# Block modulation beside w_out one chunk for one, and the first two feature tiles multiplied before their token factor

## The chip, the cores and the metric

The kernel runs on one core of one Trainium2 chip. The metric is device time in microseconds (us), the median over executions of the whole program. All tensors are fp32, and each weight matrix is read from HBM once.

## The reference, cut to what matters

One transformer layer acts on 128 context tokens and 256 latent tokens, 2048 features wide, so 384 tokens in three tiles of 128. The two groups differ in their conditioning vector (`c_ctx` or `c`), so everything that comes from the modulation exists twice, for the columns 0 to 127 and 128 to 383.

```python
mod = silu(c) @ w_mod + b_mod                  # w_mod: 2048 x 12288, six sections of 2048
shift1, scale1, gate1, shift2, scale2, gate2 = split(mod, 6)
h = rmsnorm(x, norm1) * (1 + scale1) + shift1   # rmsnorm: x * rsqrt(mean(x*x) + eps) * norm1
q, k, v, ... = split(h @ w_in)                  # w_in: 2048 x 10272
y = sigmoid(gate_a) * (y_a @ w_pa) + sigmoid(gate_b) * (y_b @ w_pb)
x = x + gate1 * (y @ w_out)                     # w_out: 2048 x 2048
h = rmsnorm(x, norm2) * (1 + scale2) + shift2
x = x + gate2 * ((silu(a) * b) @ w_down)        # a, b = halves of conv(h @ w_up)
```

The factor `rsqrt(mean(x*x) + eps)` belongs to a token and is called the factor of the tokens below. `norm1 * (1 + scale1)` and `shift1` belong to a feature.

## The kernel before, in words

**Chunks.** All weights pass through pieces of 512 KB, 128 partitions by 1024 numbers (`CK`), called chunks. A chunk is loaded on SyncE's queue (L340 to L345) into one of six buffers `raw`. Most chunks are then split in two parts: ScalarE rounds a half to fp32r (`hi`, L361), VectorE takes the rest (`lo`, L362), and TensorE makes three products of each pair of tiles, high by high, high by low and low by high (`mm3`, L370 to L373). There are five buffers for `hi` and five for `lo`. The list `chunks` is the order of the program; the loop `run` (L1246) walks it, loads up to five chunks ahead (`LD`), and splits two parts ahead (`SPL`). The compiler's scheduler then sets the order on each engine, and engines run their instructions in that order.

**The start.** SyncE's queue first takes the 18 pieces of the tokens (`xtok`, L97, 3.15 MB). The squares of all of them (`squares`, L103) give the factor of the tokens by a chain on VectorE (`rms_scale`, L189). The modulation for a feature tile of 128 (shift1 and scale1) takes four chunks of w_mod, multiplied on TensorE by `silu(c)` (`mb`, L227) and turned over through `finish` (L234). `prep_x` (L444) scales the tokens by their factor and transposes them (`sd`, L460, then `xn`), and `modulate` (L473) makes the input of the products, high part `xg` and low part `xl`.

**The first pass over w_in** makes q and k of both mixers, 24 tiles of 128 rows by 384 tokens, in nine stages by feature tiles (`STAGES`, L1116): one tile, one tile, then two at a time. Stage one and stage two have three chunks of w_in each, the later ones six. `SHARES` says after which chunk of w_in how many chunks of w_mod for the next stage stand. Each product is added from PSUM to the tile it belongs to (`evac_part`, L496): L502 and L500 copy in the first stage, L506 (VectorE, one instruction for 384 columns) and L504 add in the later ones. "Third stage" below means feature tiles 2 and 3.

**Block modulation on VectorE.** The other sections of w_mod (gate1, scale2, shift2, gate2) need no TensorE: `late_mod` (L252 to L265) multiplies each chunk by `silu(c)` on VectorE, four instructions of 128x512 for a chunk, adding into `lacc`. These are 128 chunks, 16 blocks of eight; they are called late chunks. After a block's eighth chunk `late_sum` (L287) sums over the partitions with 16 small products (L292). `spread` (L1095) puts late chunks among the main ones by a share for each phase (`dens`, L1201); `finish_late(b)` (L1195) puts all that are due and left, without main chunks between them.

**The second half.** The product by w_out goes by four column blocks of eight chunks; `spread` acts on the first five of each with share `dens[4]`. Results are gated and added to x (L924, L926), and the next block's first parts carry the second input's making (`scaled`, L944, with `hl`, L954). Then w_up goes in eleven groups of 16 chunks with share `dens[5]`, and from the third group on, after every second one, comes a group of w_down (16 chunks, products L428 to L430 with stationary `gh` and `gl`). Ahead of the first group of w_down stands `finish_late(4)` (L1228), because its gates need gate2.

Of the kernel before, what the change touches and what calls it, by code (L numbers as in the profile page):

```python
# [14 lines left out]
P = 128  # L15
# [20 lines left out]
def hybrid_step(  # L36
# [55 lines left out]
    xtok = []  # L92
    for t in range(3):
        row = []
        for (a, b) in XP:
            xt_ = slot("xtok")
            S.dma_start(out=xt_[:, :P * (b - a)], in_=xsrc[t][:, P * a:P * b])  # L97
            row.append(xt_)
        xtok.append(row)
# [3 lines left out]
    def squares():  # L103
        for t in range(3):
            for i, (a, b) in enumerate(XP):
                junk = sp.tile([P, NTOK], F32, name=nm("junk"), tag="pT", bufs=3)
                n = P * (b - a)
                if i % 3 == 2:
                    V.tensor_tensor(junk[:, :n], xtok[t][i][:, :n], xtok[t][i][:, :n], ALU.mult)
                    V.tensor_reduce(ssq1[:, t, i:i + 1], junk[:, :n], AX.X, ALU.add)  # L110
                else:
                    A.activation(junk[:, :n], xtok[t][i][:, :n], AF.Square, accum_out=ssq1[:, t, i:i + 1])
# [26 lines left out]
    squares()  # L139
# [66 lines left out]
    class Mod:  # L206
# [4 lines left out]
        def __init__(self, cols, width):  # L211
            self.cols, self.width, self.bank, self.n = cols, width, None, 0
            self.nk = CK // width
# [6 lines left out]
        def mm(self, raw, i, g):  # L220
            if self.bank is None:
                self.bank = s2p.tile([P, 2, 512], F32, name=nm("mb"), tag="sc")[:, 0]
            w = raw.rearrange("p (k c) -> p k c", k=self.nk)
# [111 lines left out]
    class Chunk:  # L335
        def __init__(self, src, shape, mm, split=True, by_rows=True):
            self.src, self.shape, self.mm, self.split, self.by_rows = src, shape, mm, split, by_rows
            self.raw, self.parts, self.need = None, [], None

        def load(self):  # L340
# [4 lines left out]
            S.dma_start(out=self.v, in_=self.src)  # L345

        def do_split(self, part):
# [12 lines left out]
            l = lo[:, :k * ncol].rearrange("p (k c) -> p k c", k=k)  # L360
            A.copy(h, v)  # L361
# [8 lines left out]
    def mm3(ps, wh, wl, xh, xl, first, last):  # L370
        T.matmul(ps, lhsT=wh, rhs=xh, start=first, stop=False)  # L371
        T.matmul(ps, lhsT=wh, rhs=xl, start=False, stop=False)  # L372
        T.matmul(ps, lhsT=wl, rhs=xh, start=False, stop=last)  # L373

# [21 lines left out]
    def partial_chunk(w, k0, nk, c0, evac):  # L396

        ncol = CK // nk

        def mm(ch, part):  # L400
            h, l = ch.parts[part]
            for i in range(ncol // P // PARTS):
                ps = mm_bank()[:, 0:NTOK]
                cs = slice(128 * i, 128 * i + 128)
                for kk in range(nk):
                    xh_, xl_ = xs1(k0 + kk)
# [34 lines left out]
    xl = [xp.tile([P, NX], R32, name=f"xl{k}", tag=f"xl{k}")[:, :NTOK] for k in range(KT)]  # L441
    xn = []

    def prep_x():  # L444
        tot = sp.tile([P, 3], F32, name="tot", tag="ssqa")
# [35 lines left out]
    def first_input(k0, nk):  # L481
        while len(xn) < k0 + nk:
            next(prep)
# [645 lines left out]
    for i, ch in enumerate(stage_mods(0)):  # L1129
        chunks.append(ch)  # L1130
        if i >= 2:
            mark(lambda: next(prep))
# [202 lines left out]
```

## Time and profile before

| what | value |
|---|---|
| median of 3 runs | 2313.24 us (2309.41 to 2313.98) |
| profiled execution, its own time | 2311.3 us |
| its span in the trace | 2309.6 us |
| TensorE busy | 2245.2 us, 97% of the span |
| VectorE busy | 1637.9 us, 71% |
| ScalarE busy | 1015.9 us, 44% |
| GpSimd busy | 146.5 us, 6% |
| chunks of w_mod, 512 KB each | 192, of them 128 late chunks |

The profiled execution lies 1.9 us under the median, inside the spread of the three runs. Times in the trace count from the start of the span; 1.7 us of the execution lie outside it. A product of 512 columns or 384 columns shows a "duration" longer than the step from one product to the next, since they are pipelined: the step is what counts in a dense stretch.

### The profile page before, as it was taken

Reading aid. Unit: us, or ns where it says so; the run is one execution under the profiler, and the core shown is the slowest. Engines: PE = TensorE matmul, PEld = TensorE weight load, DVE = VectorE, ACT = ScalarE, POOL = GpSimd, SP = SyncE. Lnnn points to the kernel's source line nnn. Section 1 sums busy time; section 2 is a strip of 40 time slices with the busy share of each in tenths; the row PEclk is TensorE's granted clock in tenths of the full one; section 3 lists DMA queues with packets and bytes.
Section 4 is the critical chain, followed back from the end, with each engine's and each line's share of the span. In section 5 each row is a group of like instructions: output and inputs, shape, how many; then the busy total and the mean of one; then the engine's idle time right before and its main releaser. Section 6 shows DMA issues by size and latency. Waiting matters only on the chain.

```text
span 2309.6 us, 34978 instructions
## 1 busy us (share of the span) xinstructions
PE 2245.2 (97%) x12814; PEld 2065.4 (89%) x12814; DVE 1637.9 (71%) x3413; ACT 1015.9 (44%) x2104; POOL 146.5 (6%) x261
## 2 busy tenths in 40 slices
PE   6999999999999999999999959999999999999998
PEld 5888997889999999987899958998899899989987
DVE  5777877777889989876789875565555555556576
ACT  5322355575555433333455522454344345434541
POOL 1000222211111100010000000000000000000000
PEclk9999999999999999999999979999999999999999
DMA  8787654445566677775656545444543543453462
GB/s 269 252 247 240 182 140 126 128 130 147 171 175 176 181 217 235 208 255 157 191 181 188 179 149 161 129 127 131 152 128 120 155 137 119 136 155 120 137 209 84
DMA packets 300300, 388.22 MB, mean 168 GB/s; under 512 B 17669, under 2 KB 215829, under 8 KB 300129
## 3 DMA queue, kind: packets, MB, share of 16 engines
q1 hardware_dynamic: 293552, 377.34, 53.6%
q0 software_dynamic: 5712, 7.09, 1.1%
q8 instruction: 100, 1.64, 0.3%
q10 hardware_dynamic: 864, 1.57, 0.2%
q14 instruction: 72, 0.58, 0.1%
HBM read 381.18 MB, written 4.76 MB: 167 GB/s over the span
## 4 chain that ended last, share of the span: by engine, by line
PE 89%; DVE 4%; DMA 3%; ACT 1%; issue 1%; POOL 0%; SPq 0%; DVEq 0%; ACTq 0%; POOLq 0%
PE mm L371 20%; PE mm L372 20%; PE mm L373 20%; PE mm L428 7%; PE mm L429 7%; PE mm L430 7%; DMA raw<-in_w_mod_dram 2%; DVE lacc L265 1%; PE mb L227 1%; DVE lo L362 1%; PE mm L1066 1%; PE mm L1065 1%; PE mm L1064 1%; PE sd L829 0%; DMA raw<-in_w_in_dram 0%
## 5 line engine op out<-in xcount | busy, mean ns | idle before, releaser
L361 ACT CAST hi<-raw 128x512 fp32r<-128x512 f32 x960 | 591.0, 620 | 1012.4 <-PE mm L372 526.4
L362 DVE TENSOR_TENSOR lo<-raw,hi 128x512 fp32r<-128x512 f32 x960 | 659.7, 693 | 482.3 <-ACT hi L361 478.3
L371 PE MATMUL mm<-hh,hi 128*128 128x386 f32 x1408 | 479.4, 340 | 0.0
L372 PE MATMUL mm<-hl,hi 128*128 128x386 f32 x1408 | 479.0, 340 | 0.0
L373 PE MATMUL mm<-hh,lo 128*128 128x386 f32 x1408 | 478.2, 340 | 0.0
L265 DVE SCALAR_TENSOR_TENSOR lacc<-raw,scT,lacc 128x512 f32<-128x512 f32 x480 | 342.0, 747 | 23.0 <-DMA raw<-in_w_mod_dram 22.8
L371 PE MATMUL mm<-xg,hi 128*128 128x384 f32 x1024 | 354.4, 347 | 2.2 <-ACT hi L361 1.4
L373 PE MATMUL mm<-xg,lo 128*128 128x384 f32 x1024 | 345.5, 337 | 0.0
L372 PE MATMUL mm<-xl,hi 128*128 128x384 f32 x1024 | 345.3, 337 | 0.0
L371 PEld LDWEIGHTS mm<-hh,hi 128*128 128x128 f32 x1408 | 267.7, 190 | 0.9 <-ACT hi L361 0.4
L372 PEld LDWEIGHTS mm<-hl,hi 128*128 128x128 f32 x1408 | 267.0, 190 | 0.2
L373 PEld LDWEIGHTS mm<-hh,lo 128*128 128x128 f32 x1408 | 266.6, 189 | 0.0
L371 PEld LDWEIGHTS mm<-xg,hi 128*128 128x128 f32 x1024 | 192.4, 188 | 21.9 <-issue 12.3
L428 PE MATMUL mm<-hi,gh 128*128 128x512 f32 x480 | 188.1, 398 | 15.3 <-ACT hi L361 14.8
L373 PEld LDWEIGHTS mm<-xg,lo 128*128 128x128 f32 x1024 | 192.2, 188 | 1.0 <-issue 0.8
L429 PE MATMUL mm<-lo,gh 128*128 128x512 f32 x480 | 190.5, 397 | 2.5 <-DVE lo L362 2.5
L372 PEld LDWEIGHTS mm<-xl,hi 128*128 128x128 f32 x1024 | 192.5, 188 | 0.5 <-issue 0.4
L430 PE MATMUL mm<-hi,gl 128*128 128x512 f32 x480 | 189.8, 395 | 0.0
L428 PEld LDWEIGHTS mm<-hi,gh 128*128 128x128 f32 x480 | 90.7, 189 | 37.1 <-ACT hi L361 15.0
L429 PEld LDWEIGHTS mm<-lo,gh 128*128 128x128 f32 x480 | 90.8, 189 | 23.8 <-DVE lo L362 3.0
L430 PEld LDWEIGHTS mm<-hi,gl 128*128 128x128 f32 x480 | 90.8, 189 | 21.5
L506 DVE TENSOR_TENSOR qk<-qk,mm 128x384 f32<-128x384 f32 x160 | 86.0, 549 | 25.0 <-PE mm L373 24.7
(333 smaller groups left out, 2974.0 us busy)
## 6 DMA issues: line engine op xcount, KB each, us to landing
raw<-in_w_mod_dram SPq DMA_DIRECT2D x192, 512.0 KB, 4.3
raw<-in_w_up_dram SPq DMA_DIRECT2D x176, 512.0 KB, 3.5
raw<-in_w_in_dram SPq DMA_DIRECT2D x160, 512.0 KB, 4.5
raw<-in_w_down_dram SPq DMA_DIRECT2D x80, 512.0 KB, 3.9
raw<-in_w_out_dram SPq DMA_DIRECT2D x32, 512.0 KB, 4.3
raw<-gate SPq DMA_DIRECT2D x28, 512.0 KB, 4.3
raw<-in_w_pb_dram SPq DMA_DIRECT2D x16, 512.0 KB, 3.8
raw<-in_w_pa_dram SPq DMA_DIRECT2D x16, 512.0 KB, 4.4
```

The costliest lines, as they stand in the source:

```text
L227: T.matmul(self.bank[32 * q:32 * q + 32, 0:self.width], lhsT=scT[:, k, 2 - 2 * i:34 - 2 * i], rhs=w[:, kk], start=i == 0 and k < 4, stop=i ...
L265: V.scalar_tensor_tensor(acc[:, j], w[:, kk], col, acc[:, j], ALU.mult, ALU.add)
L361: A.copy(h, v)
L362: V.tensor_tensor(l, v, h.bitcast(F32), ALU.subtract)
L371: T.matmul(ps, lhsT=wh, rhs=xh, start=first, stop=False)
L372: T.matmul(ps, lhsT=wh, rhs=xl, start=False, stop=False)
L373: T.matmul(ps, lhsT=wl, rhs=xh, start=False, stop=last)
L428: T.matmul(ps, lhsT=xh_[:, ts_], rhs=h[:, kk], start=k == ks[0], stop=False)
L429: T.matmul(ps, lhsT=xh_[:, ts_], rhs=l[:, kk], start=False, stop=False)
L430: T.matmul(ps, lhsT=xl_[:, ts_], rhs=h[:, kk], start=False, stop=k == ks[-1])
L506: V.tensor_tensor(dst[h][:, :NTOK], dst[h][:, :NTOK], ps, ALU.add)
L1064: T.matmul(ps, lhsT=gh[:, ts_], rhs=h, start=k == KL[0], stop=False)
```

## The change

**Late chunks.** `dens[4]` goes from .5 to 1. In the program's list of loads, before, 86 late chunks stand ahead of the first chunk of w_out, 10 between there and the first chunk of w_up, and 32 between there and the first of w_down: 24 of these stand among the chunks of w_up, and the last eight, a whole block, behind them. Now the same three numbers are 86, 20 and 22, and all 22 stand among the chunks of w_up.

**Tokens.** Only the first of six column pieces of the tokens (feature tiles 0 to 2) is loaded ahead of the weights; the other five are loaded behind chosen chunks (`then`, `load_x`). The squares of a piece are taken by ScalarE alone, behind an instruction that waits for a result of the first stages (`behind`).

**Products without the factor.** The first two feature tiles (`NRAW`) are transposed unscaled (`raw_tile`), multiplied by `norm1 * (1 + scale1)`, and get two more columns with `shift1` (`raw_input`, 386 columns in all); they are kept in the tiles of `xl` that are used last. Their products are summed over two stages, then GpSimd multiplies the 24 sums by the factor of the tokens (`times_r`), spread over the partitions by `token_row`. The third stage adds its products and the shift columns, with two VectorE instructions where one was (L573 in the changed kernel), and for the four tiles of `qa` with two more on ScalarE. The modulated inputs of tiles 0 and 1, which later phases need, are made in the third stage (`first_input(0, 2)`).

**Splits.** Among the first 20 chunks, a part is split only when its chunk is the next one, and chunks that are not split let a split happen too (`split_ahead`).

On SyncE, at the start of the program, the queue holds these loads (`xtok` are pieces of the tokens, `raw` are chunk buffers). Before:

```order
L97 DMA xtok_120<-in_x_sample_dram 128x384
L97 DMA xtok_122<-in_x_sample_dram 128x384
L97 DMA xtok_124<-in_x_sample_dram 128x128
L345 DMA raw_226<-in_w_mod_dram 128x8x128
L345 DMA raw_228<-in_w_mod_dram 128x8x128
L345 DMA raw_230<-in_w_mod_dram 128x8x128
L345 DMA raw_232<-in_w_mod_dram 128x8x128
L345 DMA raw_234<-in_w_in_dram 128x1024
```

These three loads of tokens are the last of 18. In the changed kernel the queue begins, behind the constants, with:

```order
L98 DMA xtok_90<-in_x_prompt_dram 128x384
L98 DMA xtok_92<-in_x_sample_dram 128x384
L98 DMA xtok_94<-in_x_sample_dram 128x384
L346 DMA raw_154<-in_w_mod_dram 128x8x128
L346 DMA raw_156<-in_w_mod_dram 128x8x128
L346 DMA raw_158<-in_w_mod_dram 128x8x128
L346 DMA raw_160<-in_w_mod_dram 128x8x128
L346 DMA raw_162<-in_w_in_dram 128x1024
L346 DMA raw_164<-in_w_in_dram 128x1024
L98 DMA xtok_166<-in_x_prompt_dram 128x384
```

Three loads of tokens stand ahead of the first weights instead of 18, and the next ones follow behind the second chunk of w_in.

On VectorE, at the end of w_up's third group (`z` are the convolution's results, `lacc` the sums of a block of late chunks, `lo_14833` the low part of the first chunk of w_down), before:

```order
L991 SCALAR_TENSOR_TENSOR z_14712<-u_14711,cw,z_14712 128x255
L265 SCALAR_TENSOR_TENSOR lacc_14731<-raw_14599,scT,lacc_14731 128x512 x2
L265 SCALAR_TENSOR_TENSOR lacc_14731<-raw_14633,scT,lacc_14731 128x512 x4
L265 SCALAR_TENSOR_TENSOR lacc_14731<-raw_14639,scT,lacc_14731 128x512 x4
L265 SCALAR_TENSOR_TENSOR lacc_14731<-raw_14673,scT,lacc_14731 128x512 x4
L265 SCALAR_TENSOR_TENSOR lacc_14731<-raw_14723,scT,lacc_14731 128x512 x4
L265 SCALAR_TENSOR_TENSOR lacc_14731<-raw_14729,scT,lacc_14731 128x512 x4
L265 SCALAR_TENSOR_TENSOR lacc_14731<-raw_14736,scT,lacc_14731 128x512 x4
L265 SCALAR_TENSOR_TENSOR lacc_14731<-raw_14742,scT,lacc_14731 128x512 x4
```

and six rows further on `lo_14833`. In the changed kernel (`lo_14853` is the first part of w_down there):

```order
L1061 SCALAR_TENSOR_TENSOR z_14702<-u_14701,cw,z_14702 128x255
L368 TENSOR_TENSOR lo_14790<-raw_14639,hi_14789 128x512
L1060 SCALAR_TENSOR_TENSOR z_14718<-u_14717,cw,z_14718 128x127
L1060 SCALAR_TENSOR_TENSOR z_14718<-u_14717,cw,z_14718 128x255
L1061 SCALAR_TENSOR_TENSOR z_14718<-u_14717,cw,z_14718 128x127
L1061 SCALAR_TENSOR_TENSOR z_14718<-u_14717,cw,z_14718 128x255
L368 TENSOR_TENSOR lo_14819<-raw_14673,hi_14818 128x512
L368 TENSOR_TENSOR lo_14835<-raw_14673,hi_14834 128x512
L282 TENSOR_TENSOR lev_14802<-lev_14802,brow_14856 128x128 x2
L368 TENSOR_TENSOR lo_14853<-raw_14727,hi_14852 128x512
```

The eight late chunks between w_up and w_down are gone from this place, and the first part of w_down is split right behind the last parts of w_up.

On VectorE, in the third stage of the first pass (`qk` are the 24 tiles of q and k, `mm` the products in PSUM, `xl` the low part of the third stage's input), before:

```order
L362 TENSOR_TENSOR lo_822<-raw_729,hi_821 128x512
L506 TENSOR_TENSOR qk_339<-qk_339,mm_825 128x384
L506 TENSOR_TENSOR qk_345<-qk_345,mm_833 128x384
L362 TENSOR_TENSOR lo_842<-raw_729,hi_841 128x512
L506 TENSOR_TENSOR qk_351<-qk_351,mm_845 128x384
L506 TENSOR_TENSOR qk_357<-qk_357,mm_853 128x384
```

and in the changed kernel:

```order
L368 TENSOR_TENSOR lo_839<-raw_746,hi_838 128x512
L573 SCALAR_TENSOR_TENSOR qk_260<-qk_260,mm_842 128x128
L573 SCALAR_TENSOR_TENSOR qk_260<-qk_260,mm_842 128x256
L573 SCALAR_TENSOR_TENSOR qk_266<-qk_266,mm_851 128x128
L573 SCALAR_TENSOR_TENSOR qk_266<-qk_266,mm_851 128x256
L368 TENSOR_TENSOR lo_861<-raw_746,hi_860 128x512
L573 SCALAR_TENSOR_TENSOR qk_272<-qk_272,mm_864 128x128
L573 SCALAR_TENSOR_TENSOR qk_272<-qk_272,mm_864 128x256
```

Between two splits stand four instructions instead of two.

The diff, cut to its core:

```diff
+    def load_x(i):
+        a, b = XP[i]
+        for t in range(3):
+            xtok[t][i] = slot("xtok")
+            S.dma_start(out=xtok[t][i][:, :P * (b - a)], in_=xsrc[t][:, P * a:P * b])
+    load_x(0)
-    def squares():
+    def squares(i, behind=None):
+        if behind:
+            A.copy(ssq1[:, :, i], behind()[:, 0:3])
...
     def partial_chunk(w, k0, nk, c0, evac):
+        xs, n = (xs0, NX) if k0 < NRAW else (xs1, NTOK)
...
+    def times_r(x):
+        if "r" in first:
+            G.tensor_tensor(x[:, :NTOK], x[:, :NTOK], first["r"], ALU.mult)
+        else:
+            first.setdefault("wait", []).append(x)
+    def raw_input(k):
+        if k not in x0:
+            raw_tile(k)
+        scale_of(0, 1, k, k + 1)
+        x, (h, l) = x0[k], (xlx[KT - 2 - 2 * k], xlx[KT - 1 - 2 * k])
+        x0[k] = (h, l)
+        for j, (a, b) in enumerate(SEGS):
+            A.activation(h[:, a:b], x[:, a:b], AF.Copy, scale=sc_[:, 0, k, j:j + 1])
+            V.scalar_tensor_tensor(l[:, a:b], x[:, a:b], sc_[:, 0, k, j:j + 1], h[:, a:b].bitcast(F32),
+                                   ALU.mult, ALU.subtract)
...
+        elif k0 < NRAW:
...
+            times_r(dst[h])
+        elif k0 == NRAW and dst is not qa:
+            for j, (a, b) in enumerate(SEGS):
+                V.scalar_tensor_tensor(dst[h][:, a:b], dst[h][:, a:b], dst[h][:, NTOK + j:NTOK + j + 1], ps[:, a:b],
+                                       ALU.add, ALU.add)
...
-    SHARES = ((0, 2, 2), (0, 3, 5)) + ((0, 2, 2, 2, 2, 0),) * 7
+    SHARES = ((0, 0, 4), (0, 3, 5)) + ((0, 2, 2, 2, 2, 0),) * 7
...
+            if (st, i) == (2, 3):
+                mark(lambda: first_input(0, 2))
...
+            for g in squared.get((st, i), ()):
+                mark(lambda g=g: squares(*g))
+            if (st, i) == (1, 0):
+                mark(first_scale)
...
+    for i, at in enumerate((5, 7, 9, 10, 11)):
+        early[at].then = lambda i=i: load_x(i + 1)
+    early[10].behind = early[11].behind = lambda: kb[7]
...
-    dens = (.25, .25, .75, .8, .5, .5)
+    dens = (.25, .25, .75, .8, 1, .5)
```

More of the change, by code (lines that the diff above doesn't have):

```diff
@@ L337, in __init__ @@
             self.src, self.shape, self.mm, self.split, self.by_rows = src, shape, mm, split, by_rows
-            self.raw, self.parts, self.need = None, [], None
+            self.raw, self.parts, self.need, self.then, self.behind = None, [], None, None, None
         def load(self):
@@ L440, in hybrid_step, with token_row @@
     xh = [xg[k // 4][:, k % 4] for k in range(KT)]
-    xl = [xp.tile([P, NX], R32, name=f"xl{k}", tag=f"xl{k}")[:, :NTOK] for k in range(KT)]
-    xn = []
-    def prep_x():
+    xlx = [xp.tile([P, NX], R32, name=f"xl{k}", tag=f"xl{k}") for k in range(KT)]
+    xl = [x[:, :NTOK] for x in xlx]
+    xn = {}
+    x0 = {}
+    first = {}
+    def token_row(rs):
+        ps = sd_bank()
+        for t in range(3):
+            dg = sp.tile([P, P], F32, name=nm("dg"), tag="sqj")
+            V.tensor_scalar(dg, ident, rs[:, t:t + 1], None, ALU.mult)
+            T.matmul(ps[:, 128 * t:128 * t + 128], lhsT=ones, rhs=dg, start=True, stop=True)
+        return ps[:, :NTOK]
@@ L451, in prep_x, with xs0 @@
+    def xs0(k):
+        return x0[k]
+    def prep_x():
+        rs, scaled_ = first["rs"], set()
+        for k in (2, 3, 0, 1) + tuple(range(4, KT)):
+            if k // 3 not in scaled_:
+                scaled_.add(k // 3)
                 n = P * (XP[k // 3][1] - XP[k // 3][0])
@@ L481, in first_input @@
     def first_input(k0, nk):
-        while len(xn) < k0 + nk:
+        while any(k not in xn for k in range(k0, k0 + nk)):
             next(prep)
-        scale_of(0, 1, k0, k0 + nk)
+        if k0 >= NRAW:
+            scale_of(0, 1, k0, k0 + nk)
         for k in range(k0, k0 + nk):
@@ L972, in second_scale @@
         V.memset(r[:, NTOK:NX], 1.0)
-        ps = sd_bank()
-        for t in range(3):
-            dg = sp.tile([P, P], F32, name=nm("dg"), tag="sqj")
-            V.tensor_scalar(dg, ident, rs[:, t:t + 1], None, ALU.mult)
-            T.matmul(ps[:, 128 * t:128 * t + 128], lhsT=ones, rhs=dg, start=True, stop=True)
-        A.copy(r[:, :NTOK], ps[:, :NTOK])
+        A.copy(r[:, :NTOK], token_row(rs))
     za, gs = {}, {}
@@ L1255, in loads, with split_ahead @@
                 done["load"] += 1
+        place = {id(c_): i for i, c_ in enumerate(real)}
+        FIRST = 20
+        def split_ahead(pos, n):
+            while done["split"] < min(n, len(splits)):
+                ch, p_ = splits[done["split"]]
+                if ch.raw is None or pos + 1 < place[id(ch)] < FIRST:
+                    break
+                ch.do_split(p_)
+                done["split"] += 1
         pos = at = 0
@@ L1266, in run @@
                 for part in range(PARTS):
-                    while done["split"] < min(at + 1 + SPL, len(splits)):
-                        ch, p_ = splits[done["split"]]
-                        if ch.raw is None:
-                            break
-                        ch.do_split(p_)
-                        done["split"] += 1
+                    split_ahead(pos, at + 1 + SPL)
                     due()
```

85 lines of the change are left out of this document (52 added, 33 removed).

## The prediction

> **What bounds the kernel now.** I read the first page of the profile first: shares of the engines and the 40 slices.
>
> ```profile
> PE 2245.2 (97%) x12814; PEld 2065.4 (89%) x12814; DVE 1637.9 (71%) x3413; ACT 1015.9 (44%) x2104; POOL 146.5 (6%) x261
> PE   6999999999999999999999959999999999999998
> PEclk9999999999999999999999979999999999999999
> ```
>
> TensorE (PE) is the bound. Only two of the 40 slices (57.7 us each) fall under 8: the first, with 6, and the 24th, with 5, where the granted clock falls too. The change touches both. So I looked next at the busy time by windows around 1350 us, with one window from the second change from w_up to w_down, at 1586 us, for comparison.
>
> ```profile
> core 0: us, PE busy (x) PEld busy (x) DVE busy (x) ACT busy (x) POOL busy (x), PEclk, DMA share, GB/s
> 1350.00:1360.00 10.00, 3.89 (x35) 3.37 (x33) 7.13 (x16) 3.18 (x7) 0.00 (x0) 0.91 0.02 2
> 1360.00:1370.00 10.00, 1.35 (x3) 0.83 (x3) 10.00 (x16) 1.14 (x2) 0.00 (x0) 0.50 0.69 206
> 1370.00:1380.00 10.00, 1.97 (x17) 0.82 (x16) 9.77 (x19) 3.05 (x6) 0.70 (x2) 0.50 0.66 192
> 1580.00:1590.00 10.00, 10.00 (x53) 9.27 (x52) 6.12 (x13) 5.19 (x11) 0.00 (x0) 1.00 0.38 107
> ```
>
> PE stands nearly idle from 1354 to 1380 us while VectorE (DVE) is full, and the memory moves 2 GB/s in the first of these windows. At 1586 us the same change of phase costs PE nothing. The timeline of four engines says why (PE, then DVE, ACT, and SyncE's queue):
>
> ```profile
> 1353.22 0.66 PE L292 MATMUL sd<-lacc,ones 128*32 128x128 f32 x16
> 1368.65 1.65 PE L428 MATMUL mm<-hi,gh 128*128 128x512 f32 x3 [14.76 <-ACT hi L361]
> 1376.90 1.67 PE L292 MATMUL sd<-lacc,ones 128*32 128x128 f32 x16 [6.60 <-DVE lacc L265]
> 1381.08 0.80 PE L429 MATMUL mm<-lo,gh 128*128 128x512 f32 x1 [2.50 <-DVE lo L362]
> ...
> 1385.51 0.42 PE L429 MATMUL mm<-lo,gh 128*128 128x512 f32 x1
> ...
> 1386.00 0.39 PE L428 MATMUL mm<-hi,gh 128*128 128x512 f32 x1
> 1386.23 0.40 PE L429 MATMUL mm<-lo,gh 128*128 128x512 f32 x1
> ```
> ```profile
> 1357.46 19.96 DVE L265 SCALAR_TENSOR_TENSOR lacc<-raw,scT,lacc 128x512 f32<-128x512 f32 x30
> ```
> ```profile
> 1367.98 1.14 ACT L361 CAST hi<-raw 128x512 fp32r<-128x512 f32 x2 [11.88 <-DMA raw<-in_w_down_dram]
> ```
> ```profile
> 1364.20 5.67 SPq L345 DMA_DIRECT2D raw<-in_w_down_dram  x3
> ```
>
> The block of eight late chunks holds all six chunk buffers. DVE needs 30 instructions, 19.96 us, to empty them; the first chunk of w_down can be asked for only at 1364.20, ACT splits it at 1367.98, and its low parts stand behind the late chunks in DVE's order. PE then starts at a granted clock of 0.50.
>
> **The burst is taken away.** In the changed order no late chunk stands there, and the first parts of w_down are split behind the last of w_up, as at 1586 us. What it costs now: from 1381.08 to 1385.51 stand ten products of w_down in the trace, and three stood at 1368.65, so 13 are issued by 1385.5. At the step of 0.23 us (1386.00 to 1386.23) 13 take 3.0 us. The sums L292 are done at 1353.9, and the second set of them, 0.66 us warm, stays. So the 13th would be out at 1353.9 + 0.7 + 3.0 = 1357.6: **28 us less**. Its cover is DVE's slack in w_up; if that were missing it would come back as a part of the 20 us.
>
> **Ten late chunks move into w_out.** The late chunks there go from 10 to 20. The groups of DVE over that phase, and the phase as one window:
>
> ```profile
> 988.00:1122.00 134.00, 132.92 (x622) 108.51 (x621) 95.91 (x175) 47.78 (x93) 5.54 (x12) 1.00 0.63 202
> ```
> ```profile
> L362 DVE TENSOR_TENSOR lo<-raw,hi 128x512 fp32r<-128x512 f32 x63 | 42.9, 688 | 30.5 <-ACT hi L361 30.3
> L265 DVE SCALAR_TENSOR_TENSOR lacc<-raw,scT,lacc 128x512 f32<-128x512 f32 x48 | 34.0, 745 | 5.8 <-DMA raw<-in_w_mod_dram 5.8
> L954 DVE SCALAR_TENSOR_TENSOR hl<-sd,sc__224,hh 128x128 fp32r<-128x128 f32 (+1 forms) x24 | 8.9, 411 | 0.4
> ```
>
> One late chunk costs DVE 4 x 0.67 = 2.7 us in a row (19.96 us for 30), so ten add 27 us to 96 of 134 us: 123, or 92%. On average that fits. But the late chunks stand in the first five chunks of each of four blocks, where PE takes 134/32 = 4.2 us a chunk and DVE 2 x 0.69 for the splits and 2.7 for the late one, 4.1 us. On top come, from the block before, eight instructions L954 (24 over three blocks; 3.3 us) and six that gate, 512 columns each, priced as splits (4.1 us). These 7.4 us meet a lead of two split parts, one chunk of PE, 4.2 us; 3.2 us are over, unless late chunks wait instead of splits, and the last three chunks, which have no late one, make up 8 us. DVE also waits in order for late chunks to land (5.8 us now); ten more would be about as much again. Bounds: nothing, if late chunks take all the waiting, to 3.2 us in each of three blocks, 10 us. I take **3 us more**, nearer the low end, because of the 30.5 us in which DVE waits for ACT: there ACT waits for PE to free `hi`, so DVE has its full lead. Traffic rises from 202 GB/s by 5.2 MB over 134 us to 241, under what the start reaches (324, below).
>
> **The start.** These windows and timeline rows (ACT, then PE) are the start of the program:
>
> ```profile
> 20.00:30.00 10.00, 8.98 (x74) 6.32 (x74) 3.55 (x10) 7.15 (x18) 0.00 (x0) 1.00 1.15 324
> 30.00:40.00 10.00, 10.00 (x96) 8.93 (x95) 4.29 (x11) 9.58 (x23) 0.00 (x0) 1.00 0.78 265
> 40.00:50.00 10.00, 10.00 (x76) 9.01 (x75) 7.96 (x17) 4.46 (x11) 0.00 (x0) 1.00 0.66 217
> 50.00:60.00 10.00, 8.63 (x77) 6.71 (x76) 6.96 (x16) 1.41 (x3) 0.00 (x0) 1.00 0.92 304
> ```
> ```profile
> 9.47 0.28 ACT L135 ACTIVATE scT<-sd 128x16 f32<-128x16 f32 x2
> ```
> ```profile
> 21.66 1.08 PE L227 MATMUL mb<-raw,scT 128*32 128x128 f32 x16 [0.64 <-DMA raw<-in_w_mod_dram]
> ...
> 26.64 1.15 PE L371 MATMUL mm<-xg,hi 128*128 128x384 f32 x4
> ...
> 62.90 0.62 PE L227 MATMUL mb<-raw,scT 128*32 128x256 f32 x2 [0.68 <-DMA raw<-in_w_mod_dram]
> 63.45 0.44 PE L371 MATMUL mm<-xg,hi 128*128 128x384 f32 x1
> ```
>
> The fourth chunk of w_mod is multiplied at 21.66 us behind 18 loads of tokens. Without 15 of them (2.55 MB of 3.15) it is there 2.55 MB / 0.3 MB per us = 8.5 us sooner, at 13.2; `silu(c)` is ready at 9.75, and three chunks at 1.08 us fit between. The first product moves from 26.64 to about 18 us. But the tokens must still come before the third stage, whose first product, at 63.45, stands right behind a chunk of w_mod waited for at 62.90: there the memory ends last. The bytes up to that point are the same in both kernels, so 8.5 us are not kept. What is kept is the time in which the queue now runs below its rate, because buffers wait for a late PE: from 30 to 50 us it moves 265 and 217 GB/s between neighbours of 324 and 304. The shortfall is (314 - 265 + 314 - 217) x 10 us = 1.46 MB, at 314 GB/s **4.6 us less** to the third stage. Bounds: 2 us, if half of the dip stays, to 7, if the first ten microseconds fill too.
>
> **The third stage pays back.** Its window, and DVE's group there that is split in two:
>
> ```profile
> 63.50:95.80 32.30, 32.30 (x222) 29.04 (x222) 27.17 (x56) 10.35 (x19) 0.00 (x0) 1.00 0.78 249
> ```
> ```profile
> L506 DVE TENSOR_TENSOR qk<-qk,mm 128x384 f32<-128x384 f32 x23 | 12.3, 549 | 3.0 <-PE mm L373 2.9
> ```
>
> DVE has 27.2 of 32.3 us. Twenty tiles change from one L506 (0.55 us) to a pair; the pair L954 (128 and 256 columns, mean 0.41) takes 0.82, so 20 x 0.27 = 5.4 us. The inputs of tiles 0 and 1 add six instructions of up to 384 columns, priced as L506: 3.3 us. And GpSimd (POOL) multiplies 24 tiles meanwhile. What POOL does to DVE shows where POOL rotates q and k, at 260 us: the low parts L362 of the whole run, then those of 260 to 270 us (min, median, max), and POOL's own price.
>
> ```profile
> L362 DVE TENSOR_TENSOR lo<-raw,hi x960: 654/691/1225, 24.9 to 2254.1; 128x512 fp32r<-128x512 f32 x192
> ```
> ```profile
> L362 DVE TENSOR_TENSOR lo<-raw,hi x4: 761/922/1078, 261.0 to 269.4; 128x512 fp32r<-128x512 f32 x4
> ```
> ```profile
> L523 POOL TENSOR_TENSOR qk<-qk,cst 128x256 f32<-128x256 f32 x16 | 13.5, 846 | 0.0
> ```
>
> A split takes 0.23 us more beside POOL, 0.53 at most; the 12 splits of the stage give 2.8 us, at most 6.4. DVE: 27.2 + 5.4 + 3.3 + 2.8 = 38.7 us, over the 32.3 that PE takes. Of the 6.4 over, the four PSUM banks of `mm` and the slack of the fourth stage take some. I take **4 us more**, bounds 1 and 9. POOL itself: 24 x 0.846 x 1.5 = 30 us, from about 51 us (the factor needs the last tokens and a place on PE before stage two ends) to 81; the third stage asks for the tiles in the same order until 90, so POOL is covered by some 8 us. What is late next is DVE's adding, which frees PE's banks.
>
> The Trainium skill's page "SBUF — State Buffer", section "Who interferes with whom", speaks against this step: VectorE with two SBUF inputs and GpSimd reading SBUF exclude each other, and the second waits for the whole instruction. The 1.08 us split above agrees in kind. Taken in full it is the first rival below.
>
> **Sum.** 28 + 4.6 less, 3 + 4 more: 25.6 us. Against the profiled execution of 2311.3 us that is 2285.7; the median before, 2313.24, is 1.9 higher, so 2287.6, rounded down to **2287 us**. No difference under 0.2% (4.6 us) could be told from none.
>
> **Rivals.**
> - *POOL holds DVE for whole products.* If each of the 24 products (1.27 us) cost DVE half its length, 15 us come in place of 2.8; the third stage takes 12 us longer. For it: splits of up to 1.225 us. Against: the median beside POOL is 0.92. Time: about 2299 us. Chance 0.10.
> - *w_out becomes DVE's.* Late chunks that land late and wait for `lacc`'s one buffer stop DVE in order, with the splits behind: the 10 us of the bound, 2294 us. For it: 5.8 us of waits for landing. Chance 0.15.
> - *The third stage absorbs it.* DVE's lag disappears in the slack; the start keeps 6 us and w_out costs nothing: 2280 us. Chance 0.13.
> - *Slower than before: the block's work is not hidden anywhere.* If each of the ten moved late chunks put its whole 2.7 us on PE's path, since DVE has no slack left in the first five chunks of a block, the 28 us come back as 27; with the third stage at its bound of 9 more and the start at its bound of 2 less the time is 2313.2 - 28 + 27 + 9 - 2 = 2319. It decides when DVE's demand there passes PE's 4.2 us a chunk by more than the last three chunks make up, 8 us a block. Against: 92% on average. Chance 0.03.
> - *The stall at 1354 stays*, since the last late chunks of w_up still hold buffers: 2308 us or so. Against: the order. Chance 0.02.
>
> **Numbers.** The forecast has 0.57. Its own range is 2281 to 2293. The range for 8 in 10 takes in the absorbing rival and most of w_out's: 2278 to 2297. Faster by over 0.2%: 0.96; within: 0.01; slower: 0.03.
>
> **What would show it.** Right: in the changed profile PE runs at 10.00 of 10 us through the first change from w_up to w_down, with no L265 (now L266) run of 20 us and the clock at 1.00; the first product near 18 us; the third stage starts near 59 us and lasts about 36, with DVE full. Wrong: PE gaps over 1 us at the blocks of w_out behind DVE's low parts or `lacc`; the third stage longer than 41 us; or a start of the third stage later than 62 us.

## The result, and the profile after

| | before | after |
|---|---|---|
| median | 2312.9 us (4 runs, 2309.4 to 2314.0) | 2297.4 us (4 runs, 2295.5 to 2300.0) |
| ratio | 1 | 0.9936, 95% interval 0.9919 to 0.9953 |
| profiled execution, its span | 2311.3, 2309.6 us | 2296.4, 2294.7 us |

The change is faster by some 15 us and not by 25.6. The forecast of 2287 us is missed, and its range ends 0.4 us below the median. Of the kernels further below, tokens_only, no_factor, warm and shift_dve had one execution each of 3127 to 5644 us in a slow state, which is left out of their medians. The page of after, its totals and two rows of the 40 slices:

```profile
PE 2246.3 (98%) x12826; PEld 2066.9 (90%) x12826; DVE 1643.8 (72%) x3430; ACT 1024.4 (45%) x2141; POOL 173.3 (8%) x285
PE   7899999999999999999999999999999999999998
PEclk9999999999999999999999999999999999999999
```

The 5 in the 24th slice is gone, the first slice is 7 where it was 6. The windows around the first w_down, in which PE stood nearly idle before:

```profile
1350.00:1360.00 10.00, 10.00 (x70) 9.55 (x69) 7.39 (x17) 6.65 (x14) 0.00 (x0) 1.00 0.36 107
1360.00:1370.00 10.00, 10.00 (x58) 9.96 (x57) 3.41 (x6) 3.08 (x6) 1.99 (x4) 1.00 0.39 109
1370.00:1380.00 10.00, 10.00 (x45) 8.09 (x44) 8.18 (x18) 5.95 (x12) 0.00 (x0) 1.00 0.46 138
```

PE is full and the clock is 1.00. So the loss is elsewhere. To find it I laid the phases of all traces beside each other, by the first product of each phase. Times count from the start of the span. The third stage begins with the 145th product of the first pass, since stages one and two have 72 each. `add_xstat` is the function that makes the products of the pass over w_in behind the first one. "w_out's stretch" runs from the first product of w_out to the first of w_up, and the last column from there to the first product of the next group of w_up:

| trace | first product | third stage | fourth stage | add_xstat | w_out's stretch | first w_up and w_down |
|---|---|---|---|---|---|---|
| before | 26.6 | 65.6 | 95.8 | 275.2 | 142.1 | 305.2 |
| after | 18.5 | 71.6 | 104.3 | 285.6 | 148.2 | 275.8 |
| late_only | 26.7 | 64.9 | 95.7 | 275.8 | 148.4 | 276.2 |
| tokens_only | 19.8 | 73.0 | 105.7 | 286.3 | 142.6 | 304.5 |
| late_in_up | 25.7 | 64.0 | 94.1 | 274.3 | 141.4 | 277.0 |
| no_factor | 18.9 | 64.6 | 95.8 | 276.4 | 148.3 | 275.3 |
| pool_beside | 17.9 | 69.8 | 101.2 | 282.7 | 146.8 | 275.8 |
| factor_dve | 19.5 | 76.3 | 110.2 | 288.9 | 144.7 | 275.6 |
| warm | 20.1 | 64.5 | 95.7 | 277.2 | 146.0 | 275.2 |
| squares_dve | 19.3 | 63.4 | 94.6 | 274.5 | 146.6 | 275.2 |
| no_behind | 19.8 | 67.3 | 97.7 | 278.3 | 151.2 | 275.2 |
| shift_dve | 18.6 | 71.9 | 106.6 | 286.1 | 145.3 | 275.6 |
| tokens_best | 18.5 | 76.6 | 108.5 | 289.8 | 143.9 | 276.6 |
| late_half | 26.9 | 64.9 | 95.1 | 274.6 | 144.8 | 276.2 |
| late_quarter | 26.6 | 64.5 | 94.7 | 274.5 | 143.6 | 276.1 |
| late_double | 26.6 | 65.5 | 95.7 | 274.9 | 147.7 | 305.4 |

Between before and after: 29.4 us less around the first w_down, 6.1 more in w_out, **10.4 more up to add_xstat**, and 2.1 less in later work whose order did not change (not followed up). With 0.2 more between add_xstat and w_out that is 14.8 us less, which is what the spans differ by. The start, forecast at 0.6 us less, became the largest loss. Each row is one execution, and PE's first instruction stands 7.4 to 9.3 us after the start of the span in these traces, so a difference of 1 or 2 us between two rows says little. (The expectations below count from that instruction, set to 7.53 us. Their 70.9, 63.5 and 284.9 us are 71.6, 64.6 and 285.6 in this table.)

PE's rows in after show both ends of that loss (in brackets, how long PE stood idle and for what):

```profile
18.53 1.01 PE L377 MATMUL mm<-xl,hi 128*128 128x386 f32 x2 [2.76 <-ACT xl L497]
...
71.60 0.41 PE L377 MATMUL mm<-xg,hi 128*128 128x384 f32 x1 [2.27 <-DVE qk L568]
```

The first product comes 8.1 us sooner, the third stage 6 us later. All that PE waited for from 55 to 72 us in after (us in total, times, longest), then the same from 55 to 65 us in no_factor, the changed kernel without GpSimd's products (below):

```profile
PE mm L377 <- DVE qk L566: 3.3, 3, 2.2
PE mm L377 <- DVE qk L568: 2.3, 1, 2.3
PE mm L379 <- DVE lo L368: 0.9, 1, 0.9
```
```profile
PE mb L228 <- DMA raw<-in_w_mod_dram: 0.2, 1, 0.2
```

In after that is 6.5 us, all of it for VectorE. The windows between the two ends (columns as in the prediction: PE, PEld, DVE, ACT, POOL, clock, DMA, GB/s):

```profile
20.00:30.00 10.00, 9.31 (x39) 8.98 (x39) 0.00 (x0) 7.00 (x19) 0.00 (x0) 0.75 1.11 347
30.00:40.00 10.00, 7.76 (x98) 6.92 (x97) 4.05 (x11) 9.33 (x32) 0.00 (x0) 1.00 0.66 218
40.00:50.00 10.00, 10.00 (x73) 8.99 (x72) 8.57 (x23) 6.35 (x25) 0.00 (x0) 1.00 0.80 271
50.00:60.00 10.00, 8.54 (x72) 5.40 (x70) 8.89 (x23) 6.88 (x15) 4.19 (x4) 1.00 1.04 350
60.00:70.00 10.00, 5.94 (x45) 3.40 (x44) 10.00 (x16) 3.06 (x6) 10.00 (x10) 1.00 0.59 178
70.00:80.00 10.00, 8.40 (x39) 8.43 (x40) 8.12 (x16) 3.79 (x10) 10.00 (x10) 0.83 0.48 159
```

Three things stand out. The memory still runs at 218 and 271 GB/s from 30 to 50 us, so the dip stayed. From 60 to 70 us PE has 5.94 of 10 us while DVE and POOL are both at 10.00. DVE has only 16 instructions there. In the last row the clock is 0.83: behind PE's pauses it ran at half speed again, from 72.9 us on, which takes 1.7 us of PE's work from these 10 us, inside the third stage. DVE's groups from 45 to 71 us, with the mean of one in ns behind the comma, and POOL's:

```profile
L368 DVE TENSOR_TENSOR lo<-raw,hi 128x512 fp32r<-128x512 f32 x6 | 6.4, 1093 | 0.0
L568 DVE TENSOR_TENSOR qk<-qk,mm 128x386 f32<-128x386 f32 x11 | 6.0, 551 | 0.0
L536 DVE TENSOR_SCALAR hf<-xn,sc__152,mod 128x128 f32<-128x128 f32 (+1 forms) x4 | 3.6, 968 | 0.0
...
L539 DVE TENSOR_TENSOR xl<-hf,xg 128x384 fp32r<-128x384 f32 x2 | 2.2, 1114 | 0.0
```
```profile
L477 POOL TENSOR_TENSOR qk<-qk,r 128x384 f32<-128x384 f32 x24 | 27.1, 1165 | 46.7 <-ACT r L471 46.7
```

A split that takes 0.69 us elsewhere takes 1.09 on average (1.51 at most). The input of the third stage (`hf`, then `xl`) takes 2.6 and 2 times as long as it does without POOL (rows of no_factor, below).

### The profile page after: what moved, and what is told of

The parts are those of the page before. It is cut to its first block, busy times and chain, and to the rows that moved or that the text cites. A ratio compares the mean times of both kernels' runs of the same rounds, so it can differ in the third digit from the quotient of the medians.

```text
span 2294.7 us, 35120 instructions
## 1 busy us (share of the span) xinstructions
PE 2246.3 (98%) x12826; PEld 2066.9 (90%) x12826; DVE 1643.8 (72%) x3430; ACT 1024.4 (45%) x2141; POOL 173.3 (8%) x285
## 4 chain that ended last, share of the span: by engine, by line
PE 88%; DVE 5%; DMA 3%; issue 1%; ACT 1%; POOL 0%; DVEq 0%; ACTq 0%; POOLq 0%
PE mm L377 20%; PE mm L378 20%; PE mm L379 20%; PE mm L438 7%; PE mm L439 7%; PE mm L440 7%; DMA raw<-in_w_mod_dram 2%; DVE lacc L266 1%; DVE lo L368 1%; PE mb L228 1%; DMA raw<-in_w_out_dram 1%; PE mm L1136 1%; DMA raw<-in_w_in_dram 1%; PE mm L1135 1%; PE mm L1134 1%
## 5 line engine op out<-in xcount | busy, mean ns | idle before, releaser
L378 PE MATMUL mm<-xl,hi 128*128 128x384 f32 (+1 forms) x1024 | 347.4, 339 | 0.1
L377 PE MATMUL mm<-xg,hi 128*128 128x384 f32 x976 | 338.4, 347 | 3.4 <-DVE qk L568 2.3
L379 PE MATMUL mm<-xg,lo 128*128 128x384 f32 x976 | 330.0, 338 | 0.0
L377 PEld LDWEIGHTS mm<-xg,hi 128*128 128x128 f32 x976 | 183.7, 188 | 21.5 <-issue 15.2
L379 PEld LDWEIGHTS mm<-xg,lo 128*128 128x128 f32 x976 | 183.7, 188 | 1.1 <-issue 0.8
L438 PE MATMUL mm<-hi,xg 128*128 128x256 f32 (+1 forms) x288 | 96.7, 336 | 0.0
```

The lines of the kernel that those rows point to most:

```text
L438: T.matmul(ps, lhsT=xh_[:, ts_], rhs=h[:, kk], start=k == ks[0], stop=False)
```

## The experiments

Each ratio stands against the kernel before on the same chip (medians 2311.1 to 2311.5 us there, 2312.9 beside after). So where a run is compared with after, the difference is taken from the ratios, in parts of 2311 us.

**The two halves apart: late_only and tokens_only.** late_only is the kernel before with one edit, tokens_only is the changed kernel with the opposite one:

```
-    dens = (.25, .25, .75, .8, .5, .5)
+    dens = (.25, .25, .75, .8, 1, .5)
```

> The kernel before with w_out's share of late chunks set to one to one, and nothing else. If the two halves of the change simply add, this one leaves out the start's loss of 9.7 us that the two traces show (add_xstat's first product 275.2 to 284.9 us) and keeps the 6.0 us lost in w_out and the 29.4 us won around the first w_down: 2313 - 29.4 + 6.0 = about 2289 us. Rival: the 6.0 us of w_out come from the token half (what the first stages leave behind), so they go too: 2284 us. Second rival: the start's loss is made up later in any case, and this kernel is no better than the changed one: 2297 us.

> The changed kernel with w_out's share of late chunks put back to one to two: the start alone. If the halves add: 2313 + 9.7 = about 2322 us, with PE's stall before the first w_down back. Rival (the w_out loss belongs to this half): 2328 us. Second rival (made up later): 2313 us.

Measured: late_only 2287.5 us (ratio 0.990, 0.9887 to 0.9913), tokens_only 2320.7 us (1.0042, 1.0027 to 1.0057). The halves add: 23.7 less and 9.5 more make 14.2 less, where the whole change gave some 15. The second half of the change alone is slower than doing nothing, and the w_out loss stays with the late chunks (148.4 against 142.6 us).

**The late chunks in w_up: late_in_up.** The kernel before, with `dens = (.25, .25, .75, .8, .5, .69)`.

> The kernel before with w_out's share left at one to two and the share of the three first groups of w_up raised from .5 to .69, so that the 8 chunks of the burst go among w_up's products and none is added to w_out. Theory (a late chunk costs only where VectorE has no slack, and w_up's first groups have it: VectorE busy 174 of 206 us there, and 8 chunks of four operations of 0.744 us add 24): the 29 us come in full and no 6 us are lost, 2284 us. Rival (VectorE at 198 of 206 us makes TensorE wait as in w_out, 0.6 us a chunk or more): 2289 to 2294 us, with gaps on TensorE between 1144 and 1350 us.

Measured: 2281.8 us (0.987, 0.9857 to 0.9884), the fastest of all kernels here that compute everything. PE's windows at the change to w_down, and w_up's first three groups as one window:

```profile
1345.00:1355.00 10.00, 10.00 (x68) 9.20 (x66) 7.62 (x15) 4.75 (x10) 0.00 (x0) 1.00 0.73 250
1355.00:1365.00 10.00, 10.00 (x45) 8.11 (x44) 7.31 (x17) 4.54 (x8) 1.99 (x4) 1.00 0.32 108
```
```profile
1143.00:1351.80 208.80, 208.80 (x1216) 206.88 (x1215) 196.05 (x387) 109.66 (x217) 10.40 (x22) 1.00 0.64 199
```

The 32 late chunks in w_up cost 1.2 us more than the 22 of after (277.0 and 275.8), and w_out keeps its 141.4. The theory holds: breaking up the burst was enough. Its reason, that w_up has slack, needs a second look: VectorE is busy 196 of 208.8 us there, 94%, and PE has no gap. After's w_out, as one window, has more slack and loses time:

```profile
1012.60:1160.80 148.20, 141.94 (x666) 112.18 (x665) 121.11 (x219) 52.59 (x103) 4.21 (x9) 1.00 0.66 210
```

VectorE is busy 82% here, and PE stands for 6.3 us. The average load does not say where late chunks are cheap.

**The price of POOL's products: no_factor.** In `times_r` the instruction is left out, so that q and k lack the factor in the first two tiles' products.

```
-            G.tensor_tensor(x[:, :NTOK], x[:, :NTOK], first["r"], ALU.mult)
+            pass
```

> The changed kernel without GpSimd's 24 products (the factor of the tokens is left out of q and k from the first two tiles; all else is issued as before). Theory (the products beside VectorE set when the third stage starts, through VectorE's operations at 1 to 1.5 us in place of 0.4 to 0.7, and ScalarE's 7.1 us wait for a product): third stage from 70.9 back to about 64 us, and some 3 us less within it: 2288 us. Rival (the stage is late because of what came before: TensorE at half clock from 18 to 25 us, squares on ScalarE, loads held up until 47 us): third stage still at 69 to 71 us, and the time within 2 us of the changed kernel, 2296 us.

Measured: 2284.5 us (0.9885, 0.987 to 0.990), 11.8 less than after by the ratios. The third stage starts at 64.6 instead of 71.6. DVE's groups from 45 to 66 us:

```profile
L568 DVE TENSOR_TENSOR qk<-qk,mm 128x386 f32<-128x386 f32 x14 | 7.4, 551 | 0.1
L368 DVE TENSOR_TENSOR lo<-raw,hi 128x512 fp32r<-128x512 f32 x6 | 3.9, 686 | 0.0
...
L536 DVE TENSOR_SCALAR hf<-xn,sc__152,mod 128x128 f32<-128x128 f32 (+1 forms) x4 | 1.2, 376 | 0.0
...
L539 DVE TENSOR_TENSOR xl<-hf,xg 128x384 fp32r<-128x384 f32 x2 | 1.0, 552 | 0.0
```

Six splits, four `hf` and two `xl` take 6.1 us and not 12.2: 6.1 of the 7.0 us by which the stage is earlier. The theory holds, and its price was too small.

**Contention or waiting: pool_beside.** POOL does 24 products that nobody waits for, on a tile of its own:

```
-            G.tensor_tensor(x[:, :NTOK], x[:, :NTOK], first["r"], ALU.mult)
+            G.tensor_tensor(first["r2"], first["r"][:, :376], first["r"][:, :376], ALU.mult)
```

> The changed kernel in which GpSimd's 24 products work on a tile that nobody else reads or writes (r times r, 376 of the 384 columns; the factor is left out of q and k, as in no_factor): the same work beside the same VectorE, but no engine waits for a product. Theory (contention alone: GpSimd's products beside VectorE's operations stretch them): third stage at about 70 us, first product of add_xstat at about 284 us, time 2294 to 2297 us. Rival (the waits for the products do it: ScalarE stood 7.1 us before a shift whose q tile was still to be multiplied, and the splits and loads behind it with it): third stage at 64 us, time 2285 to 2287 us.

Measured: 2293.2 us (0.992, 0.9908 to 0.9932), 8.1 more than no_factor by the ratios, third stage at 69.8. POOL's group and the splits from 55 to 84 us (min, median, max; then the same for no_factor):

```profile
L478 POOL TENSOR_TENSOR r<-r x24: 814/816/1397, 56.4 to 80.2; 128x376 f32<-128x376 f32 x24
```
```profile
L368 DVE TENSOR_TENSOR lo<-raw,hi x10: 675/818/1299, 57.2 to 82.3; 128x512 fp32r<-128x512 f32 x10
```
```profile
L368 DVE TENSOR_TENSOR lo<-raw,hi x12: 681/685/693, 56.7 to 83.2; 128x512 fp32r<-128x512 f32 x12
```

Contention alone gives two thirds of the 11.8 us, with products that are shorter here than the real ones. The clock is 1.00 here from 70 to 80 us, so by estimate 1.7 us of the remaining third is after's half clock in that stretch. The rest was not split between the products' greater length and the waits.

**The wait on ScalarE: shift_dve.** In after, ScalarE stands before a shift of `qa` until POOL has multiplied that tile:

```profile
75.24 0.80 ACT L578 ACTIVATE qk<-qk 128x128 f32<-128x128 f32 x2 [7.14 <-POOL qk L477]
```

```
-                    A.activation(dst[h][:, a:b], dst[h][:, a:b], AF.Identity, bias=...)
+                    V.tensor_scalar(dst[h][:, a:b], dst[h][:, a:b], ..., None, ALU.add)
```

> The changed kernel, factor on GpSimd, with the eight shift additions of the four qa tiles on VectorE in place of ScalarE, so that ScalarE's splits do not stand 7.1 us behind a product of GpSimd's. If that wait matters beside the contention: the loads and splits from 68 to 80 us come earlier, the third stage lasts some 3 us less, 2294 us. Rival (VectorE is busy without a break there and now does the waiting itself): no gain, 2297 us, or slower by the 8 operations, 2300 us.

Measured: 2293.5 us (0.9921, 0.9908 to 0.9934), 3.5 less than after by the ratios, whose intervals overlap. That is the theory's 2294 us, but by luck. The start did not improve: the third stage lasts 34.7 against 32.7 us, and add_xstat comes at 286.1 against 285.6. The difference lies in w_out's stretch (145.3 against 148.2), which this edit does not touch and which scatters by more than that (below). Taking away ScalarE's longest wait there did not shorten the start.

**Another engine: factor_dve.** `G.tensor_tensor` in `times_r` becomes `V.tensor_tensor`.

> The changed kernel with the 24 products by the factor issued on VectorE in place of GpSimd. Theory (what cost 12 us was GpSimd's 24 x 1.13 us beside a VectorE that is busy without a break): VectorE gets 24 operations of about 0.55 us, 13 us, 16 of them ahead of the third stage's input, 8.8 us, but its own operations go back to 0.4 and 0.7 us: third stage at 63.5 + 8.8 = about 72 us and the time within 3 us of the changed kernel, 2294 to 2300 us. Rival (the engine does not matter, the place in the order does: GpSimd's queue made ScalarE and the loads wait): the time falls half way to that without products, to about 2291 us.

Measured: 2299.2 us (0.9946, 0.9933 to 0.9958). DVE's groups from 55 to 84 us:

```profile
L477 DVE TENSOR_TENSOR qk<-qk,r 128x384 f32<-128x384 f32 x24 | 11.7, 546 | 0.0
L368 DVE TENSOR_TENSOR lo<-raw,hi 128x512 fp32r<-128x512 f32 x7 | 4.7, 676 | 0.0
```

The splits are back at 0.68 us, 11.7 us of products stand in DVE's order, and the time is after's within the intervals (2.3 us more by the ratios). So on POOL the products cost about as much time as on DVE itself. The theory holds for the time and the splits. The third stage came later than it said, at 74.5 in its counting and not at 72, in an execution that is the fastest of the five (2293.9 us).

**What else holds the start back: warm, squares_dve, no_behind.** All three start from no_factor, whose third stage stands at 64.6, 1.0 us ahead of before's, though the first product is 7.7 us ahead. warm keeps PE busy ahead of the first product; squares_dve takes squares from ScalarE, and no longer holds the second piece's squares behind a result of the first stage (`(1, lambda: qb[7])` becomes `(1, None)`); no_behind drops a copy that holds the second stage's modulation.

```
+        ps = sd_bank()
+        for i in range(12):
+            T.matmul(ps[:, 0:128], lhsT=ident, rhs=ident, start=True, stop=True)
```
```
+            if i < 2:
+                V.tensor_tensor(junk[:, :n], xtok[t][i][:, :n], xtok[t][i][:, :n], ALU.mult)
+                V.tensor_reduce(ssq1[:, t, i:i + 1], junk[:, :n], AX.X, ALU.add)
+                continue
```
```
-        return Mod([D + P * k0, P * k0], P * nk, (lambda: kb[7]) if i == 1 else None).chunks()
+        return Mod([D + P * k0, P * k0], P * nk, None).chunks()
```

> The changed kernel without the factor's products (the factor is left out, as in no_factor), and with 12 products of 128x128 by the unit matrix put on TensorE between the last modulation product of the first stage (15.4 us) and the first product of q, k (17.8 us), where TensorE sat idle for 2.8 us; their result is used by nobody. Theory (the granted clock of .50 from 18 to 25 us is a debt that the first chunk pays and all later steps inherit): clock 1.00 in that window, the second chunk of products starts at 22 and not at 25.2 us, the third stage at about 60.5 and not at 63.5 us, time 2285 - 3 = 2282 us. Rival (ScalarE's copies and squares, 4.6 to 5 us busy of every 5 from 25 to 40 us, and the loads set the pace from 28 us on): the first chunks come earlier, the third stage does not move by 1 us: 2285 us.

> The changed kernel without the factor's products (as in no_factor), and with the squares of the first two of the six token groups on VectorE, idle from 20 to 33 us, in place of ScalarE: 6 x 0.7 = 4.2 us fewer there. Theory (ScalarE sets the first stage's pace after 25 us: the second stage's modulation waits until 33.4 us for its copy behind the last q, k copy): that modulation 3 to 4 us earlier, third stage from 63.5 to about 60.5 us, 2282 us. Rival (the loads set it: w_mod's and w_in's tiles of the second stage are asked for when buffers come free): no move of the third stage by 1 us, 2285 us.

> The changed kernel without the factor's products (as in no_factor), and without the one-column copy from the last k tile into the bank of the second stage's modulation, so that this modulation need not wait until 33.4 us. Theory (that copy holds the second stage's tiles of w_mod in their buffers, and so the loads of the third stage's, asked for only at 34.3 us): the modulation done by 30 us, the loads 4 us earlier, third stage from 63.5 to 59 or 60 us, 2281 us. Rival (ScalarE, full from 25 to 45 us, sets the pace, the copy only names the moment): no move by 1 us, 2285 us.

Measured: warm 2280.9 us (0.9871, 0.9856 to 0.9886), squares_dve 2281.9 (0.9874, 0.9859 to 0.9889), no_behind 2285.5 (0.9889, 0.9876 to 0.9902). warm and squares_dve come out at their theories' 2282 us. But the intervals overlap no_factor's, so the phases have to decide. In warm the clock came back sooner:

```profile
15.00:20.00 5.00, 4.60 (x24) 4.41 (x25) 3.80 (x11) 2.90 (x7) 0.00 (x0) 0.66 1.16 323
20.00:25.00 5.00, 5.00 (x31) 5.00 (x30) 0.00 (x0) 3.46 (x8) 0.00 (x0) 1.00 1.13 319
```

yet the third stage stands at 64.5: the clock's slow stretch at 18 us is not on the path. squares_dve moves it to 63.4, 1.2 us and not 3: ScalarE is a small part at most. no_behind has it at 67.3, 2.7 us later, in the slowest of its four executions (2288.9 us), and its median is not the theory's 2281: that theory falls, and why the stage is later was not followed. What stays in no_factor is SyncE's queue, which stands before full buffers:

```profile
36.69 10.69 SPq L346 DMA_DIRECT2D raw<-in_w_mod_dram  x5
47.47 4.69 SPq L346 DMA_DIRECT2D raw<-in_w_in_dram  x2
```

What its loads waited for most from 28 to 66 us, in no_factor and then in before (total, times, longest):

```profile
SPq L346 <- PE mb L228: 23.6, 11, 7.5
```
```profile
SPq L345 <- DVE lo L362: 14.2, 4, 4.4
SPq L345 <- PE mb L227: 10.6, 10, 4.6
```

In the changed start the buffers are held by chunks of w_mod until PE has multiplied them. An earlier first product does not free those.

**All of it together: tokens_best.** The changed start with the factor on POOL, the edits of squares_dve and no_behind, and late_in_up's `dens`.

> The changed start with its factor on GpSimd, the squares of two token groups on VectorE and no copy ahead of the second stage's modulation, and the late chunks as in late_in_up (one to two in w_out, .69 in the first groups of w_up): does the start, with what was found, come below the start of the kernel before? Theory (contention on VectorE costs 10 us, whatever is won ahead of it is 3 to 6 us): late_in_up's 2281.8 + 10 - 3 to 6 = 2286 to 2289 us, slower than late_in_up. Rival (an earlier start moves the products out of VectorE's full stretch): 2278 to 2282 us.

Measured: 2295.0 us (0.9932, 0.992 to 0.9944), slower than late_in_up by 13.3 us and than the theory's 2286 to 2289. Its third stage starts at 76.6, 5 us later than in after; why was not followed. With the same late chunks, the start as before wins.

**What a late chunk costs in w_out: late_half, late_quarter, late_double.** late_half and late_quarter are late_only with a half or three quarters of the multiply-adds of the late chunks in w_out left out; late_double is the kernel before with them done twice. The loads are not changed. The comments in this cut name the run.

```
+                if j and kg and (blk, kg) in half:            # late_half
+                    continue
+                if (j or kk) and kg and (blk, kg) in half:    # late_quarter
+                    continue
+                    if (blk, kg) in half:                     # late_double, after the multiply-add
+                        V.scalar_tensor_tensor(acc[:, j], w[:, kk], col, acc[:, j], ALU.mult, ALU.add)
```

> The kernel before with w_out's share of late chunks at one to one (late_only), which leaves out half of the multiply-adds of the 20 late chunks in w_out (the second of the two rows of scT, except in the first chunk of a block); their loads are all there. Theory (the 6 us lost in w_out are VectorE's 4 x 0.744 us per late chunk, which make the gating at the end of a block late): TensorE's gaps of 1.3 to 2.3 us in w_out go and the time is 2287.5 - 5 = 2283 us. Rival (they are the loads': 20 tiles of w_mod in place of 10 in the same stretch, and VectorE waits for them): the gaps stay, 2287 us.

> late_only (late chunks one to one in w_out) with one of the four multiply-adds of each of its 20 late chunks left, except in the first chunk of a block; all loads are there. In the six kernels with one to one w_out's products take 144.7 to 148.4 us from first product to w_up's, in the kernels with one to two 141.4 to 142.6. Theory (VectorE's work makes the difference): at most 143 us here, in spite of all loads. Rival (the loads of w_mod make it): 145 to 148 us.

> The kernel before (late chunks one to two in w_out), whose ten late chunks in w_out have every multiply-add but a block's first issued twice: VectorE's work of the one-to-one kernel, about 25 us more, with ten loads in place of twenty. Theory (VectorE's work): w_out's stretch 145 to 148 us in place of 142, and the time 3 to 6 us over the kernel before. Rival (loads): 142 to 143 us, and the time of the kernel before.

Measured: 2286.4 us (0.9891, 0.9877 to 0.9904), 2283.7 us (0.9889, 0.9872 to 0.9905), 2315.9 us (1.0023, 1.0012 to 1.0034). late_half told nothing apart: its time is nearer the rival's 2287 than the theory's 2283, the nine traces with w_out's full one-to-one work have 144.7 to 151.2 us there, and it has 144.8. The other two do. w_out as one window, of before, late_quarter and late_double:

```profile
1002.00:1144.00 142.00, 140.92 (x650) 111.98 (x649) 97.71 (x180) 51.19 (x100) 0.00 (x0) 1.00 0.58 184
```
```profile
1002.00:1144.00 142.00, 139.91 (x659) 111.24 (x658) 87.17 (x165) 51.05 (x100) 4.21 (x9) 1.00 0.66 215
```
```profile
1002.00:1144.00 142.00, 138.05 (x625) 109.58 (x624) 113.51 (x204) 48.70 (x94) 0.00 (x0) 0.98 0.52 170
```

With DVE at 113.5 us and half the loads the stretch takes 147.7 us; with all the loads and DVE at 87 it takes 143.6. The four traces with one to two have 141.4 to 143.9. So DVE's work makes most of the 6 us; a share of the loads is not shown. Each is one execution, but late_double's median is also clear of before's.

## Why the prediction was wrong, point by point

- **The burst, 28 us less: right.** Measured 29.4 in the profiles and 23.7 in late_only, which pays w_out's 6 out of it.
- **Ten late chunks in w_out, 3 us more: sized too small**, 6.1 measured, inside the bounds of 0 and 10. The reason named, DVE's demand, is what late_double shows. Of the 6.3 us in which PE stands, 4.1 are behind the gating at a block's end (L1001), the longest 1.6 us, and a mean load under 100% did not exclude them. The window taken for the phase lay 14 us early (988 to 1122, where w_out's products run from 1002.0 to 1144.1), which changed little: DVE has 97.8 of 142.1 us in the right one. The waits of after from 1005 to 1165 us (total, times, longest):

```profile
DVE lacc L266 <- DMA raw<-in_w_mod_dram: 7.5, 6, 1.6
...
PE sd L1023 <- DVE x1t L1001: 4.1, 3, 1.6
```

- **The third stage's start, 4.6 us less: failed.** The prediction took the product at 63.45 us for the third stage's first. Counted, it belongs to stage two, and the stage begins here:

```profile
65.65 0.34 PE L371 MATMUL mm<-xg,hi 128*128 128x384 f32 x1
```

So 61 was forecast in this counting, 71.6 came, and no_factor gives 64.6. The first 3.6 us of the miss, those of no_factor, go with the dip: the step took it that the queue would run at 314 GB/s from 30 to 50 us once the first product came sooner. It ran at 218 and 271, a shortfall of (96 + 43) x 10 us = 1.39 MB, 4.4 us, as before (4.6), since buffers still came free late: they waited for the products of w_mod, 23.6 us in no_factor. That filling the dip would have brought these 3.6 us is reckoned, not shown. The other 7.0 us are POOL's.
- **POOL beside DVE: the step that failed most.** It stood in the sum as 2.8 us for the 12 splits of the third stage. The runs price it at 11.8 us in time, 7.0 of them ahead of that stage, where PE waited 6.5 us for VectorE. Two faults: the median of four splits at 260 us was taken for a stretch in which POOL works without a pause, and only splits were counted, none of the `hf`, `xl` and small operations on the path. "POOL is covered by some 8 us" held for VectorE's additions, which waited 0.3 us for its results, and not for ScalarE, which stood 7.14 us before a shift; and it said nothing of POOL's neighbour.
- **The third stage, 4 us more: right in kind**, 2.5 (32.7 against 30.2), and 1.0 without the products. By estimate the half clock from 72.9 us on, which the sum did not have, takes 1.7 of the 2.5.
- **The rivals.** "POOL holds DVE for whole products" had 2299 us and a chance of 0.10, and it is what happened: 2297.4. It charged 12 us to the third stage, and 7 came ahead of it. That its number lies so near is luck in part: the 4.6 us less that it kept did not come, and w_out cost 3 us more than it took. "w_out becomes DVE's" came by 6.1 of its 10 us. The others did not come, the slower one included: no late chunk put its whole work on PE's path. The Trainium skill's page "SBUF — State Buffer", section "Who interferes with whom", names VectorE's operations with two SBUF inputs, and copies, casts and `tensor_scalar` in some modes, as those that contend with GpSimd. The traces agree operation by operation: splits (0.69 to 1.09 us), `xl` (0.55 to 1.11) and the `tensor_scalar` of `hf` (0.38 to 0.97) stretch, and L568, which reads PSUM and one SBUF tile, stays at 0.551 in both. Only four of its 13 from 45 to 84 us in after ran beside POOL, at 0.544 each; L573, which also reads PSUM, has twelve beside it, at 0.34 and 0.47 (0.35 and 0.48 in no_factor). Whether `hf` ran in one of those modes no run here shows. Held against the list of operations on the path, the rule would have deserved the larger chance.

## What to carry to other kernels

Work put on GpSimd is free only if VectorE has slack, or runs operations that do not stretch (here those that read PSUM), while it lasts: list VectorE's operations on the path in that window and price each beside GpSimd. An earlier first product is worth little by itself (7.7 us of it made 1.0 us at the third stage in no_factor); what counts is the next point where something is late, here the third stage's input, and the wait that ends last there. When a burst of side work stalls a change of phase, spread it out, and do not choose the place by the average load of the engine that does it: VectorE at 94% in w_up left TensorE without a gap, and at 82% in w_out it cost 6 us. In these traces TensorE's gaps stood where it needed a result of VectorE next, behind the gating at the end of a block.

## What was unexpected of the hardware

After 2.76 us without work TensorE ran at half clock for 6.5 us, though it had work almost all of that time (products of 386 columns 0.32 us apart from 20.5 to 25.0 us, 0.18 after). In warm, filler from 15.7 us on took that time over and the clock was 1.00 from 20 us. The slow stretch came earlier there, and it was shorter: a mean of 0.66 from 15 to 20 us is 3.4 us at half clock, and 0.85, 0.50 and 0.97 in the three windows of 5 us from 15 us on are 6.8 us in no_factor.

GpSimd pays for the company too: the same product of 128x384 took 989 to 1469 ns in after (1012 at 78.55 us, with no VectorE operation beside it), and one of 376 columns with one operand read twice 814 to 1397.
